# The mixer stage of a two-layer trunk: transposes by whole PSUM banks, decay matrices for two chunks at once, and other costs in the list that orders the work

## The chip, the cores and the metric

One core of one Trainium2 chip runs the whole program. The metric is the device time of one execution in microseconds. The program has five queues of instructions: PE (TensorE; its weight loads are a row of their own, PEld), DVE (VectorE), ACT (ScalarE), POOL (GpSimd) and SP (SyncE, which issues nearly all DMAs). Each queue runs in the order in which the kernel wrote it, and an instruction waits on a semaphore where it needs another engine's result.

## The reference

Layer 0 of the trunk is a state-space mixer over 256 context and 1024 latent tokens; layer 1 is an attention mixer. The change touches layer 0 alone. Its core, for each direction (forward and reversed), with tokens in chunks of 128 and heads in 8 groups `g` of 4:

```python
zc, xc, bc, cc, dtc = project(h_ctx)   # h @ in_w, a 5-tap convolution, silu
la_cum = jnp.cumsum(dtc * a, axis=2)
to_end = jnp.exp(la_cum[:, :, -1:] - la_cum) * dtc
states = jnp.einsum('bcsgn,bcsgr,bcsgrp->bcgrpn', bc, to_end, xc)
...
decay = jnp.exp(jnp.where(causal, seg, -jnp.inf))
cb = jnp.einsum('bclgn,bcsgn->bclsg', cc, bc)
w = cb[..., None] * decay * dtc[:, :, None]
y_diag = jnp.einsum('bclsgr,bcsgrp->bclgrp', w, xc)
y_off = jnp.einsum('bclgn,bcgrpn,bclgr->bclgrp', cc, prev, jnp.exp(la_cum))
```

`y_diag + y_off` of both directions, plus a skip term, is gated by `silu(z)`, normalised and multiplied by `out_w`.

## The kernel before

**Tiles.** All 1280 tokens are resident as two rounded parts, `inh` and `inl`. The projection makes 48 column tiles of 128 channels (32 that are convolved, 16 of `z`). For each it runs three token blocks of 256, 512 and 512, eight `kt` steps, and at each step three matmuls (`mm3`, lines 168 to 170: high by high, low by high, high by low), all into a `pj` bank of PSUM, of which there are two. ACT empties the bank (line 636 for a convolved tile, line 660 for `z`), four DVE taps (line 645) make the convolution, and ACT applies silu.

**A group's mix** (`mix`, one for each of the 8 groups once its tiles x0, x1, B and C are convolved) has these parts, all in plain float32 on PE:

- `trans`: for each of the ten chunks three transposes (line 690: two of x, one of B) into one `tc` bank; ACT or DVE copies x out to `xst` (lines 695, 697), ACT copies B to `Bt` (line 701). The ring `tc` has two banks.
- `state`: POOL scales x (`xw`, line 713), PE multiplies it with B (`st`, line 718), POOL decays the running state (`tm`, line 732) and DVE adds (`PV`, line 736).
- `wmat`: for one chunk, SP brings the row sums (`lab`, a ring of three tiles), POOL masks them (line 754), ACT takes eight exponentials (line 760) into W0 and W1, one for each direction; DVE adds W1 to W0 (line 773); PE makes the cross product `cb` (line 770, into a `tc` bank); DVE multiplies W0 by it (line 775). At every second chunk PE runs `diag` for both (line 795, into `yd`). W0 and W1 have two buffers each, of one chunk.
- `y_out`: PE multiplies the states with C (`yo`, line 837), DVE weighs (line 841), POOL or DVE adds (line 854), and a DMA stores.

**What sets the order.** Every step is recorded as `plan.op(engine, f, after, rank, us, takes, uses, table)`. `Plan.order` then walks a clock of its own: each engine, when it is free, takes the ready step of the lowest rank; a step is ready when its `after` steps have ended (plus `LINK`, .5 us, from another engine) and its ring has a free buffer; a step with another `table` than the engine's last costs a rank penalty and a time (`SWITCH`: 15 ranks and .2 us on PE). The result is one fixed list for each queue. The planner's times never run on the chip: there, waits come from the tiles alone. Before the change no PE step names a table.

```python
SWITCH = {"ACT": (8., 1.28), "PE": (15., .2)}
LINK, MOVE, LAND = .5, .9, 2.6
...
if any(a.end is None or a.end + (0. if a.eng == e else LINK) > now + 1e-9 for a in o.after):
    continue
```

After the mixer the program goes on with the output product, layer 1 and the final norm; their order is made by other plans, which the change leaves alone.

Of the kernel before, what the change touches and what calls it, by code (L numbers as in the profile page):

```python
# [42 lines left out]
ANY = ("tc", "wparts", "pj", "sc", "dn", "tr", "ob", "sq", "ss", "xn", "rot", "xd")  # L43
BORD = (1, 0, 9, 8, 7, 6, 5, 4, 3, 2)
# [7 lines left out]
class Plan:  # L52
# [3 lines left out]
    def __init__(self, rings):  # L56
        self.free, self.ops, self.turns, self.given = dict(rings), [], {}, {}
# [24 lines left out]
    def order(self):  # L82
# [5 lines left out]
        busy, table, moved, now, started, events = {e: 0. for e in todo}, {}, 0., 0., [], [0.]  # L88
        ends = []
        while any(todo.values()):  # L90
# [6 lines left out]
            for e, q in todo.items():  # L97
# [3 lines left out]
                for o in q:  # L101
                    if best and o.rank > best[0]:
                        break
                    if any(a.end is None or a.end + (0. if a.eng == e else LINK) > now + 1e-9 for a in o.after):
                        continue
                    if any(self.free[h.ring] <= i or h.ring not in ANY and h.n != self.given.get(h.ring, 0) + i + 1
                           for h, i in o.takes):
                        continue
                    r = o.rank + (SWITCH[e][0] if o.table and o.table != table.get(e) else 0.)
                    if best is None or r < best[0]:  # L110
                        best = (r, o)
# [4 lines left out]
                for h, _ in o.takes:  # L116
                    self.free[h.ring] -= 1
                    self.given[h.ring] = h.n
                us = o.us
                if o.table and o.table != table.get(e):  # L120
                    table[e], us = o.table, us + SWITCH[e][1]
# [7 lines left out]
                for x in (busy[e], o.end, o.end + LINK):  # L129
                    heapq.heappush(events, x)  # L130
# [15 lines left out]
def emit(tc, A, out):  # L146
# [108 lines left out]
    for b in ub:  # L255
# [5 lines left out]
                 "st": 1, "yd": 1, "yo": 1, "xst": 1, "Bt": 1, "PV": 1, "xw": 3, "tm": 1, "lab": NLAB, "W0": 2, "W1": 2, "es": 3})  # L261
# [325 lines left out]
    def load(src, after=(), rank=0., raws="wraw"):  # L587
# [18 lines left out]
        a = plan.op(*(("POOL", low, [a], rank - 30, 1.44) if odd else ("DVE", low, [a], rank - 30, .80)),  # L606
# [3 lines left out]
    def project(ct, rank):  # L610

        w = [load(A["w_in"][ct, :, h * 512:(h + 1) * 512], rank=rank + .1 * h) for h in range(2)]
        for b, (lo, hi) in enumerate(NBLK):
# [10 lines left out]
            for kt in range(KT):  # L624
                last = plan.op("PE", lambda kt=kt, f=product: f(kt), [last, w[kt // 4][2], ready_in[b, kt]], rank + .01 * b,
                               .69 if hi - lo > 256 else .36, takes=[bank] if kt == 0 else [], uses=[bank, w[kt // 4][1]])
            yield lo, hi, t, bank, last

    def conv_tile(ct, rank):
# [18 lines left out]
        for k in range(1, 5):  # L648
            a = plan.op("DVE", lambda k=k: tap(k), [a], rank - URGENT, 1.70, uses=[u, out])
# [15 lines left out]
    def mix(g, chs, rank):  # L665
# [15 lines left out]
        def trans(n, c):  # L681
            t0, bank, t = tok0(c), plan.hold("tc"), {}

            def turn():
                if n == 0:
                    s["xst"] = pool["now"].tile([128, NT, 4, 64], FT, tag="xst", name="xst")
                    s["Bt"] = pool["now"].tile([128, NT, 128], FT, tag="Bt", name="Bt")
                t["p"] = psum("tc", [128, 3, 128])
                for j, x in enumerate((x0, x1, bt)):
                    T.transpose(t["p"][:, j, :], x["a"][:, t0:t0 + 128], ident)  # L690

            def xcopy():
                xd = s["xst"][:, c].rearrange("p h d -> p (h d)")
                if n % 2 == 0:
                    S.activation(xd, flat(t["p"][:, 0:2]), AF.Copy)
                else:
                    V.tensor_copy(xd, flat(t["p"][:, 0:2]))

            a = op("PE", turn, [ax0, ax1, ab] + third, .33, takes=[bank] + ([hxst, hBt] if n == 0 else []), uses=[hx0, hx1, hb, hxst, hBt])
            b = op("DVE" if n % 2 else "ACT", xcopy, [a], .42 if n % 2 else .38, uses=[bank, hxst])  # L700
            d = op("ACT", lambda: S.activation(s["Bt"][:, c, :], t["p"][:, 2, :], AF.Copy), [a], .275, uses=[bank, hBt])
            ready[c] = (b, d)

        pv, held = [None], []

        def state(i):
            bank, t, mms = plan.hold("st"), {}, []
            for d, c in ((0, i), (1, BORD[i])):
                hw = plan.hold("xw")

                def scale(d=d, c=c):
                    t[d] = pool["now"].tile([128, 4, 64], FT, tag="xw", bufs=3, name="xw")
                    G.tensor_tensor(t[d], s["xst"][:, c], te_t[:, d, c, h4][:, :, None].to_broadcast([128, 4, 64]), op=OP.mult)  # L713

                def product(d=d, c=c):
                    if d == 0:
                        t["st"] = psum("st", [128, 2, 4, 64])
                    T.matmul(flat(t["st"][:, d]), s["Bt"][:, c, :], flat(t[d]), start=True, stop=True)  # L718

                a = op("POOL", scale, [ready[c][0], te_op], .80, takes=[hw], uses=[hxst])  # L720
                mms.append(op("PE", product, [a, ready[c][1]] + mms, .44, takes=[bank] if d == 0 else [], uses=[bank, hw, hBt]))
# [5 lines left out]
            else:  # L727
# [7 lines left out]
                a = op("POOL", decay, [pv[0]] + dec_ops, 1.11, takes=[ht], uses=[hPV])  # L735
# [3 lines left out]
        def wmat(c):  # L739

            t0, t, ws, bank = tok0(c), {}, [], plan.hold("tc")
            for d in range(2):
                hl, hw = plan.hold("lab"), plan.hold(f"W{d}")
                sgn = 1 - 2 * d

                def bring(d=d):
                    t["l", d] = pool["now"].tile([128, 4, 128], FT, tag="lab", bufs=NLAB, name="lab")
                    src = bass.AP(tensor=la_d.tensor, offset=la_d.offset + (c * 64 + d * 32 + g * 4) * 128,
                                  ap=[[0, 128], [1, 512]])
                    Q.dma_start(flat(t["l", d]), src)  # L750


                def close(d=d, sgn=sgn):
                    G.affine_select(t["l", d], t["l", d], [[0, 4], [sgn, 128]], OP.is_ge, NEVER, base=0,  # L754
                                    channel_multiplier=-sgn)

                def expo(h, d=d):
                    if h == 0:
                        t["w", d] = pool["now"].tile([128, 4, 128], FT, tag=f"W{d}", bufs=2, name="W")
                    S.activation(t["w", d][:, h], t["l", d][:, h], AF.Exp, bias=u_t[:, d, c, 4 * g + h:4 * g + h + 1])  # L760

                a = op("SP", bring, third + [la_op], .38, takes=[hl])
                a = op("POOL", close, [a], .88, uses=[hl])
                for h in range(4):
                    a = op("ACT", lambda h=h, f=expo: f(h), [a, u_op], .312, takes=[hw] if h == 0 else [], uses=[hl, hw], table="exp")
                ws.append((hw, a))

            def cross():
                t["cb"] = psum("tc", [128, 128])
                T.matmul(t["cb"], bt["a"][:, t0:t0 + 128], ct["a"][:, t0:t0 + 128], start=True, stop=True)  # L770

            b = op("PE", cross, [ab, ac], .22, takes=[bank], uses=[hb, hc])
            a = op("DVE", lambda: V.tensor_tensor(t["w", 0], t["w", 0], t["w", 1], op=OP.add), [w[1] for w in ws], .75,
                   uses=[w[0] for w in ws])
            a = op("DVE", lambda: V.tensor_tensor(t["w", 0], t["w", 0], t["cb"][:, None, :].to_broadcast([128, 4, 128]),
                                                  op=OP.mult), [a, b], .68, uses=[ws[0][0], bank])
            bi = [i for i, (c0, c1) in enumerate(BLOCKS) if c0 <= c < c1][0]
            held.append((c, t, a, ws[0][0]))
            if c % 2 == 0:
                return  # L780

            new, two = bi not in blocks, held[:]
            held.clear()
# [3 lines left out]

            def diag():
                if new:
                    bk["yd"] = [psum("yd", [128, 512]) for q in range(2)]  # L790
                for c, t, _, _ in two:
                    k = (c - bk["c"][0]) * 128
                    for h in range(4):
                        q, j = divmod(h, 2)
                        T.matmul(bk["yd"][q][j * 64:(j + 1) * 64, k:k + 128], s["xst"][:, c, h, :], t["w", 0][:, h, :], start=True,  # L795
                                 stop=True)

            bk["ops"].append(op("PE", diag, [x for c, _, w, _ in two for x in (w, ready[c][0])], 1.08, takes=[bk["h"]] if new else [],
                                uses=[bk["h"], hxst] + [x[3] for x in two]))

# [14 lines left out]
        def y_out(bi, q):  # L815
# [4 lines left out]
            for d in range(2):  # L820
# [23 lines left out]
                a = op("PE", outer, [pv[0], ac], .23 * len(cs), takes=[hy], uses=[hPV, hc])  # L844
# [3 lines left out]
                if bi == 0:  # L848
                    eng, E, us = "DVE", V, .30
# [14 lines left out]
        for n, c in enumerate(order):  # L864
            trans(n, c)
        for i in range(9):
            state(i)
            wmat(i)
# [4 lines left out]
        wmat(9)  # L873
# [13 lines left out]
    def mod_later(n, q, rank):  # L887
# [3 lines left out]
        for kt in (2 * q, 2 * q + 1):  # L891
# [13 lines left out]
            for j in both:  # L905
                done[0] = plan.op("DVE", lambda j=j, f=add: f(j), [a, done[0]], rank, .92, uses=[raw])
# [10 lines left out]
        for j in both:  # L917
# [26 lines left out]
            a = plan.op("DVE", plus, [b, done[0]], rank, .70, uses=[hr])  # L944
# [9 lines left out]
    for kind, g, q in ORDER:  # L954
# [6 lines left out]
        if q == 3:  # L961
            mix(g, chs[g], rank + 1)
    with tc.manual_schedule():
# [936 lines left out]
```

## Time and profile before

| | us |
|---|---|
| median of 3 runs | 2009.88 |
| lowest and highest run | 2005.18, 2011.53 |
| the profiled execution | 2010.66 |
| its span, first to last instruction | 2008.9 |
| granted TensorE clock in it | 0.994 |

In the profile the mixer stage reaches from the program's start to the last `yo` product at 1010 us; the first 200 us of it load, normalise and compute the step sizes, and from 200 us on the eight mixes run between the projections. Idle time of an engine is listed with what ended it. A matmul's row shows its whole passage through the array, so rows of one stream overlap: the distance from start to start is what one costs.

### The profile page before, as it was taken

Reading aid. Unit: us, or ns where it says so; the run is one execution under the profiler, and the core shown is the slowest. Engines: PE = TensorE matmul, PEld = TensorE weight load, DVE = VectorE, ACT = ScalarE, POOL = GpSimd, SP = SyncE. Lnnn points to the kernel's source line nnn. Section 1 sums busy time; section 2 is a strip of 40 time slices with the busy share of each in tenths; the row PEclk is TensorE's granted clock in tenths of the full one; section 3 lists DMA queues with packets and bytes.
Section 4 is the critical chain, followed back from the end, with each engine's and each line's share of the span. In section 5 each row is a group of like instructions: output and inputs, shape, how many; then the busy total and the mean of one; then the engine's idle time right before and its main releaser. Section 6 shows DMA issues by size and latency. Waiting matters only on the chain.

```text
span 2008.9 us, 30605 instructions
## 1 busy us (share of the span) xinstructions
PE 1949.9 (97%) x10728; PEld 1497.8 (75%) x10728; DVE 1437.8 (72%) x1737; ACT 1116.9 (56%) x2047; POOL 1189.4 (59%) x973
## 2 busy tenths in 40 slices
PE   8899999999999999999999999999999999999998
PEld 8778888888888788888878878877775444444476
DVE  1485897786959786866445788768575888888643
ACT  2446767676766677676734676534224444554521
POOL 1201776666846576856459787855265667776722
PEclk9999999999999999999999999999999999999999
DMA  6114463635372545445586686553232111111033
GB/s 244 64 32 124 132 189 115 182 100 168 112 195 91 157 125 165 141 142 158 150 278 212 212 252 196 167 153 99 74 110 90 34 41 43 43 48 32 6 105 105
DMA packets 162126, 255.50 MB, mean 127 GB/s; under 512 B 21466, under 2 KB 57178, under 8 KB 161972
## 3 DMA queue, kind: packets, MB, share of 16 engines
q1 hardware_dynamic: 160820, 251.71, 40.5%
q8 instruction: 84, 1.38, 0.3%
q10 hardware_dynamic: 1152, 1.84, 0.3%
q14 instruction: 70, 0.57, 0.1%
HBM read 210.78 MB, written 42.63 MB: 126 GB/s over the span
## 4 chain that ended last, share of the span: by engine, by line
PE 75%; DVE 9%; DMA 5%; POOL 4%; issue 3%; ACT 3%; SPq 1%; DVEq 0%; POOLq 0%; ACTq 0%
PE pj L168 8%; PE pj L169 8%; PE pj L170 8%; PE sc L1663 7%; PE ot L1679 7%; PE ob L168 7%; PE ob L170 6%; PE ob L169 6%; DVE acc L645 4%; PE yo L837 2%; PE sc L1462 2%; PE st L718 2%; DMA spare<-in_mod_w 2%; PE yd L795 2%; PE sc L168 2%
## 5 line engine op out<-in xcount | busy, mean ns | idle before, releaser
L168 PE MATMUL pj<-inh,whi 128*128 128x512 f32 (+1 forms) x1152 | 441.7, 383 | 3.9 <-DVE dv L453 3.2
L170 PE MATMUL pj<-inh,wlo 128*128 128x512 f32 (+1 forms) x1152 | 410.7, 357 | 0.0
L169 PE MATMUL pj<-inl,whi 128*128 128x512 f32 (+1 forms) x1152 | 409.9, 356 | 0.8 <-POOL inl L367 0.8
L168 PEld LDWEIGHTS pj<-inh,whi 128*128 128x128 f32 x1152 | 219.1, 190 | 32.1 <-DVE dv L453 3.6
L645 DVE SCALAR_TENSOR_TENSOR acc<-ub,convw,acc 128x1282 f32<-128x1282 f32 x128 | 230.9, 1804 | 16.3 <-ACT acc L642 13.2
L170 PEld LDWEIGHTS pj<-inh,wlo 128*128 128x128 f32 x1152 | 218.2, 189 | 32.0
L169 PEld LDWEIGHTS pj<-inl,whi 128*128 128x128 f32 x1152 | 219.4, 190 | 26.5 <-POOL inl L367 1.2
L760 ACT ACTIVATE W<-lab,u_t 128x128 f32<-128x128 f32 x640 | 202.6, 390 | 62.5 <-POOL lab L754 39.7
L754 POOL TENSOR_SCALAR_AFFINE_SELECT lab<-lab 128x512 f32<-128x512 f32 x160 | 144.8, 911 | 147.3 <-DMA lab<-la_d 141.0
L1644 POOL TENSOR_TENSOR acc<-acc,P 128x1024 f32<-128x1024 f32 x80 | 192.5, 2406 | 64.4 <-ACT P L1668 62.7
L1668 ACT ACTIVATE P<-sc 128x1024 f32<-128x1024 f32 x160 | 162.9, 1025 | 115.4 <-PE sc L1663 106.4
L1609 DVE TENSOR_REDUCE mx<-sc 128x2 f32<-128x1024 f32 (+1 forms) x140 | 167.3, 1213 | 38.3 <-PE sc L1462 37.4
L713 POOL TENSOR_TENSOR xw<-xst,te_t 128x256 f32<-128x256 f32 x144 | 143.1, 1011 | 41.5 <-PE st L718 17.8
L1679 PE MATMUL ot<-P,vv 128*64 128x512 f32 x640 | 154.8, 605 | 0.0
L602 POOL TENSOR_TENSOR wlo<-wraw,whi 128x512 fp32r<-128x512 f32 x48 | 71.7, 1493 | 126.0 <-ACT whi L599 125.8
L1663 PE MATMUL sc<-q,kh 64*128 64x512 f32 x640 | 135.9, 420 | 0.5
L170 PE MATMUL ob<-whi,yl 128*128 128x512 f32 x288 | 113.5, 394 | 1.8 <-DVE yl L1061 1.8
L168 PE MATMUL ob<-whi,yh 128*128 128x512 f32 x288 | 114.2, 397 | 0.0
L169 PE MATMUL ob<-wlo,yh 128*128 128x512 f32 x288 | 113.3, 393 | 0.0
L1663 PEld LDWEIGHTS sc<-q,kh 64*128 64x128 f32 x640 | 60.0, 184 | 69.7 <-DVE mx L1609 29.6
L902 DVE SCALAR_TENSOR_TENSOR macc<-mraw,cc,macc 128x512 f32<-128x512 f32 x98 | 102.4, 1069 | 9.9 <-DMA mraw<-in_mod_w 9.8
L732 POOL TENSOR_TENSOR tm<-PV,dec_t 128x512 f32<-128x512 f32 x64 | 92.9, 1452 | 18.3 <-DVE PV L736 17.0
(281 smaller groups left out, 4504.6 us busy)
## 6 DMA issues: line engine op xcount, KB each, us to landing
lab<-la_d SPq DMA_DIRECT2D x160, 256.0 KB
wraw<-in_w_in SPq DMA_DIRECT2D x96, 256.0 KB
workvv<-in_m_out_w SPq DMA_DIRECT2D x94, 256.0 KB
mraw<-in_mod_w SPq DMA_DIRECT2D x64, 256.0 KB
es<-e_d SPq DMA_DIRECT2D x128, 128.0 KB
wraw<-in_wqkv SPq DMA_DIRECT2D x48, 256.0 KB
spare<-in_mod_w SPq DMA_DIRECT2D x32, 256.0 KB
q_d<-qs SPq DMA_DIRECT2D x64, 128.0 KB
```

The source lines that it names most:

```text
L168: T.matmul(o, lh, rh, start=first, stop=False)
L169: T.matmul(o, lh, rl, start=False, stop=False)
L170: T.matmul(o, ll, rh, start=False, stop=last)
L645: V.scalar_tensor_tensor(t["a"], ub[i % 2][:, k:k + CW], convw[:, ct, k:k + 1], t["a"], op0=OP.mult, op1=OP.add)
L713: G.tensor_tensor(t[d], s["xst"][:, c], te_t[:, d, c, h4][:, :, None].to_broadcast([128, 4, 64]), op=OP.mult)
L754: G.affine_select(t["l", d], t["l", d], [[0, 4], [sgn, 128]], OP.is_ge, NEVER, base=0, channel_multiplier=-sgn)
L760: S.activation(t["w", d][:, h], t["l", d][:, h], AF.Exp, bias=u_t[:, d, c, 4 * g + h:4 * g + h + 1])
L1609: V.tensor_reduce(max_place(t["m"][0], i), o, AX.X, OP.max)
L1644: E.tensor_tensor(t[e], t["P", k0] if two else t[e], t["P", kt], op=OP.add)
L1663: T.matmul(o[:, h], (first_row[r] if n == 3 else (kh, kl, kh)[n][r, kv, k]), x[(0, 0, 1, 2)[n]][r], start=(n == 0), stop=(n == 3))
L1668: S.activation(t["P", kt], flat(t["s", kt]), AF.Exp)
L1679: T.matmul(t["o"][h * 64:(h + 1) * 64], vv[:, kt, kv], t["P", kt][:, h * 512:(h + 1) * 512], start=(kt == 0), stop=(kt == NT - 1))
```

## The change

1. `trans` makes five turns for x and three for B instead of ten: an x turn transposes two tiles of two chunks into one whole bank, and one copy of 512 columns empties it; a B turn takes four chunks (two in the last) and ACT copies them at once. `xst` and `Bt` now stand in the order of the transposes (`at`). An x turn no longer needs B.
2. `wmat` handles two chunks: W0 and W1 are tiles of two chunks with one buffer each, the reversed direction's exponentials stand first, one DVE add and one multiply work on 1024 columns, and one `tc` bank takes both cross products. In the plan the cross products wait for the third of the four sets of exponentials.
3. In the plan, PE steps are marked `parts` (the projection) or `whole` (the float32 steps of the mix); a change of kind costs 4 ranks and .08 us.
4. In the plan, a hand-over to PE takes 1.2 us instead of .5, the banks of ring `tc` are given out in turn (a step is not ready until the bank whose turn it is is free; before, any free bank would do in the plan), and several steps have other times: the convolution tap 1.70 to 1.8, `xw` .80 to 1.07, `tm` 1.11 to 1.5, the mask .88 to 1.0, the DVE half of a weight split .80 to 1.0, and some smaller ones.

```diff
+        self.link = {}
...
-                    if any(a.end is None or a.end + (0. if a.eng == e else LINK) > now + 1e-9 for a in o.after):
+                    if any(a.end is None or a.end + (0. if a.eng == e else self.link.get(e, LINK)) > now + 1e-9 for a in o.after):
...
-                 "st": 1, "yd": 1, "yo": 1, "xst": 1, "Bt": 1, "PV": 1, "xw": 3, "tm": 1, "lab": NLAB, "W0": 2, "W1": 2, "es": 3})
+                 "st": 1, "yd": 1, "yo": 1, "xst": 1, "Bt": 1, "PV": 1, "xw": 3, "tm": 1, "lab": NLAB, "W0": 1, "W1": 1, "es": 3})
...
-                               .69 if hi - lo > 256 else .36, takes=[bank] if kt == 0 else [], uses=[bank, w[kt // 4][1]])
+                               .69 if hi - lo > 256 else .36, takes=[bank] if kt == 0 else [], uses=[bank, w[kt // 4][1]], table="parts")
...
-            a = plan.op("DVE", lambda k=k: tap(k), [a], rank - URGENT, 1.70, uses=[u, out])
+            a = plan.op("DVE", lambda k=k: tap(k), [a], rank - URGENT, 1.8, uses=[u, out])
...
+                t[key] = psum("tc", [128, len(cs), len(tiles), 128])
+                for i, c in enumerate(cs):
+                    for j, x in enumerate(tiles):
+                        T.transpose(t[key][:, i, j, :], x["a"][:, tok0(c):tok0(c) + 128], ident)
...
-                a = op("POOL", scale, [ready[c][0], te_op], .80, takes=[hw], uses=[hxst])
+                a = op("POOL", scale, [ready[c][0], te_op], 1.07, takes=[hw], uses=[hxst])
...
-                a = op("POOL", decay, [pv[0]] + dec_ops, 1.11, takes=[ht], uses=[hPV])
+                a = op("POOL", decay, [pv[0]] + dec_ops, 1.5, takes=[ht], uses=[hPV])
...
+            done, two = [], (c0, c0 + 1)
+            for d in (1, 0):
...
+            a = op("DVE", lambda: V.tensor_tensor(t["w", 0], t["w", 0], t["w", 1], op=OP.add), done, 1.46, uses=hw)
+            b = op("PE", cross, [ab, ac, done[2]], .44, takes=[bank], uses=[hb, hc], table="whole")
+            a = op("DVE", weigh, [a, b], 1.22, uses=[hw[0], bank])
...
+    plan.switch["PE"] = (4., .08)
+    plan.link["PE"] = 1.2
```

Two places in PE's list show what this does to the order. The first is the start of group 0's mix. Before, with `tc<-ident,acc` the transposes and `pj` the projection's matmuls:

```order
L690 MATMUL tc<-ident,acc 128x128 x3
L168 MATMUL pj<-inh,whi 128x512
L169 MATMUL pj<-inl,whi 128x512
L170 MATMUL pj<-inh,wlo 128x512
L690 MATMUL tc<-ident,acc 128x128 x3
L168 MATMUL pj<-inh,whi 128x512
```

And at that place now (lines have moved: 702 is the transpose, 173 to 175 are the projection, 744 is `st`):

```order
L702 MATMUL tc<-ident,acc 128x128 x8
L173 MATMUL pj<-inh,whi 128x512
L174 MATMUL pj<-inl,whi 128x512
L175 MATMUL pj<-inh,wlo 128x512
L702 MATMUL tc<-ident,acc 128x128 x8
L173 MATMUL pj<-inh,whi 128x512
```

Two banks' worth of transposes now stand together, and three projection matmuls stand between such pairs.

The second is the last pair of chunks of group 4, with `tc<-acc` the cross product and `yo` the product with the states. Before:

```order
L837 MATMUL yo<-acc,PV 128x128
L168 MATMUL pj<-inh,whi 128x512
L169 MATMUL pj<-inl,whi 128x512
L170 MATMUL pj<-inh,wlo 128x512
L168 MATMUL pj<-inh,whi 128x256
L169 MATMUL pj<-inl,whi 128x256
L170 MATMUL pj<-inh,wlo 128x256
L770 MATMUL tc<-acc 128x128
L837 MATMUL yo<-acc,PV 128x128
```

And now (868 is `yo`, 803 the cross product):

```order
L173 MATMUL pj<-inh,whi 128x512
L174 MATMUL pj<-inl,whi 128x512
L175 MATMUL pj<-inh,wlo 128x512
L868 MATMUL yo<-acc,PV 128x128
L803 MATMUL tc<-acc 128x128 x2
L173 MATMUL pj<-inh,whi 128x512
```

Both cross products stand together now. Behind them come 18 projection matmuls before this pair's `diag`, and no other cross product. Before, at 32 of the 40 `diag` steps one or two cross products of the next pair stood ahead of the `diag`.

Over the stage PE's list has as many instructions as before. Stretches of float32 work between projection matmuls are 280 before and 243 now. ACT has 83 instructions fewer, 11 of them table loads, and DVE 104 fewer; POOL and SP have as many as before.

More of the change, by code (lines that the diff above doesn't have):

```diff
@@ L88, in order @@
         busy, table, moved, now, started, events = {e: 0. for e in todo}, {}, 0., 0., [], [0.]
+        size, out = dict(self.free), {r: [] for r in self.free}
         ends = []
@@ L679, in mix @@
         order = (0, 1, 9, 2, 8, 3, 7, 4, 6, 5)
[L681 to L690, printed above, removed]
+        at = {c: n for n, c in enumerate(order)}
@@ new lines, in trans, with turn @@
+        def trans(n):
+            t = {}
+            def turn(key, tiles, cs):
+                if not cs[0]:
+                    if key == "x":
+                        s["xst"] = pool["now"].tile([128, NT, 4, 64], FT, tag="xst", name="xst")
+                    else:
+                        s["Bt"] = pool["now"].tile([128, NT, 128], FT, tag="Bt", name="Bt")
+                t[key] = psum("tc", [128, len(cs), len(tiles), 128])
+                for i, c in enumerate(cs):
+                    for j, x in enumerate(tiles):
+                        T.transpose(t[key][:, i, j, :], x["a"][:, tok0(c):tok0(c) + 128], ident)
+            cs, bank = order[2 * n:2 * n + 2], plan.hold("tc")
+            p = op("PE", lambda: turn("x", (x0, x1), cs), [ax0, ax1, s.get("x")] + third, .45, takes=[bank] + ([] if n else [hxst]),
+                   uses=[hx0, hx1, hxst], table="whole")
+            s.setdefault("x", p)
@@ L700, in trans @@
[L700 to L704, printed above, removed]
+                    V.tensor_copy(o, i)
+            xo = op("DVE" if n % 2 else "ACT", xcopy, [p], .68 if n % 2 else .6, uses=[bank, hxst])
+            if n % 2 == 0:
+                cb, bank2 = order[2 * n:2 * n + 4], plan.hold("tc")
+                p = op("PE", lambda: turn("b", (bt,), cb), [ab, s.get("b")] + third, .11 * len(cb), takes=[bank2] + ([] if n else [hBt]),
+                       uses=[hb, hBt], table="whole")
+                s.setdefault("b", p)
+                d = op("ACT", lambda: S.activation(flat(s["Bt"][:, 2 * n:2 * n + len(cb)]), t["b"].rearrange("p c x t -> p (c x t)"),
+                                                   AF.Copy), [p], .15 * len(cb), uses=[bank2, hBt])
+                for c in cb:
+                    ready[c] = [None, d]
@@ L733, in decay @@
                                     op=OP.mult)
-                a = op("POOL", decay, [pv[0]] + dec_ops, 1.11, takes=[ht], uses=[hPV])
+                a = op("POOL", decay, [pv[0]] + dec_ops, 1.5, takes=[ht], uses=[hPV])
                 pv[0] = op("DVE", lambda: V.tensor_tensor(s["PV"][:, i], t["tm"], t["st"], op=OP.add), [a] + mms, .68,
                            uses=[ht, hPV, bank])
[L739 to L766, printed above, removed]
-            def cross():
[L769 to L783, printed above, removed]
@@ L794, in diag @@
                         q, j = divmod(h, 2)
[L795 to L799, printed above, removed]
+                        T.matmul(bk["yd"][q][j * 64:(j + 1) * 64, k:k + 128], s["xst"][:, at[c], h, :], t["w", 0][:, n, h, :],
+                                 start=True, stop=True)
+            bk["ops"].append(op("PE", diag, [a] + [ready[c][0] for c in two], 1.08, takes=[bk["h"]] if new else [],
+                                uses=[bk["h"], hxst, hw[0]], table="whole"))
         def inner(bi):
```

81 lines of the change are left out of this document (59 added, 22 removed).

## The prediction

> **What bounds the kernel now.** I read the page's first part, then busy time by stage, then PE's waits in the mixer stage, then single waits in the timeline.
>
> ```profile
> span 2008.9 us, 30605 instructions
> PE 1949.9 (97%) x10728; PEld 1497.8 (75%) x10728; DVE 1437.8 (72%) x1737; ACT 1116.9 (56%) x2047; POOL 1189.4 (59%) x973
> ```
>
> PE is busy for 97% of the span. The change reorders the mixer stage only, and of that mainly 200 to 1010 us (the row gives the stretch, its length, busy us of PE, PEld, DVE, ACT and POOL, PE's granted clock, the DMA share and GB/s):
>
> ```profile
> 200.00:1010.00 810.00, 794.66 (x4843) 677.54 (x4842) 620.86 (x722) 567.48 (x1151) 522.69 (x463) 1.00 0.49 146
> ```
>
> PE is busy there for 794.66 of 810 us at full clock, DVE for 77%, ACT 70%, POOL 65%. PE's list has the same instructions after the change, so the gain lies in what PE loses between them: 15.3 us of plain idle time, and what hides under the modelled ends of matmuls. Who ends the waits of PE's matmuls in this stretch (total, times, longest):
>
> ```profile
> PE tc L770 <- DVE W L775: 4.9, 6, 1.2
> PE st L718 <- POOL xw L713: 4.8, 5, 2.5
> PE yo L837 <- DVE es L841: 2.6, 5, 1.1
> PE st L718 <- DVE PV L736: 1.6, 3, 1.1
> PE tc L690 <- DVE xst L697: 0.7, 2, 0.4
> PE tc L690 <- ACT mr L939: 0.3, 1, 0.3
> ```
>
> And those of its weight loads:
>
> ```profile
> PEld tc L770 <- DVE W L775: 8.9, 12, 1.6
> PEld st L718 <- POOL xw L713: 7.0, 6, 2.9
> PEld yo L837 <- DVE es L841: 5.3, 7, 1.5
> PEld st L718 <- DVE PV L736: 3.7, 6, 1.4
> PEld tc L690 <- DVE xst L697: 1.5, 2, 0.8
> PEld tc L690 <- ACT Bt L701: 1.0, 4, 0.4
> PEld tc L690 <- ACT mr L939: 0.5, 1, 0.5
> ```
>
> They sum to 14.9 us in 22 waits by the matmuls and 27.9 us in 38 by the weight loads. All are short and all stand before float32 work; none names the projection. One of them in the timeline, the cross product of group 4 whose rows are in the section on the change:
>
> ```profile
> 668.76 0.69 DVE L773 TENSOR_TENSOR W<-W 128x512 f32<-128x512 f32 x1 [2.76 <-ACT W L760]
> 668.83 0.28 PE L169 MATMUL pj<-inl,whi 128*128 128x256 f32 x1
> 668.95 0.28 PE L170 MATMUL pj<-inh,wlo 128*128 128x256 f32 x1
> 669.49 0.69 DVE L775 TENSOR_TENSOR W<-W,tc 128x512 f32<-128x512 f32 x1
> 670.23 0.49 PE L770 MATMUL tc<-acc 128*128 128x128 f32 x2 [1.00 <-DVE W L775]
> ```
>
> A 256-column matmul costs .12 us from start to start (668.83 to 668.95), so PE was free at 669.07 and began at 670.23: 1.16 us lost, where the matmul's wait says 1.00. The truth lies between the two sums; I take the middle, **21.4 us** as the whole prize in this stretch. The wait is for the bank of an earlier cross product, which line 775 releases at 670.18; PE starts .05 us later. So a hand-over itself is cheap, and the wait comes from a DVE that ran late against the plan.
>
> **Kept together: the price of a change of kind.** The next rows are PE's: three and six transposes between projection matmuls.
>
> ```profile
> 620.85 0.49 PE L690 MATMUL tc<-ident,acc 128*128 128x128 f32 x3
> 621.09 0.48 PE L168 MATMUL pj<-inh,whi 128*128 128x512 f32 x1
> 621.41 0.39 PE L169 MATMUL pj<-inl,whi 128*128 128x512 f32 x1
> 621.64 0.39 PE L170 MATMUL pj<-inh,wlo 128*128 128x512 f32 x1
> ...
> 611.34 0.82 PE L690 MATMUL tc<-ident,acc 128*128 128x128 f32 x6
> 611.91 0.48 PE L168 MATMUL pj<-inh,whi 128*128 128x512 f32 x1
> 612.23 0.40 PE L169 MATMUL pj<-inl,whi 128*128 128x512 f32 x1
> ```
>
> From the first transpose to the second projection matmul it is .56 us with three and .89 us with six: .11 for each transpose. Take three transposes (.33) off .56, and .23 is left for L168, which is what a 512-column matmul of the stream costs (621.41 to the next at 621.64), so a change of kind costs at most .02 us. The list has 37 float32 stretches fewer: 37 x .02 = .7 us at most; I take .4. This part of the change hardly does what its name says.
>
> **Later and better-timed hand-overs.** A float32 step now enters PE's list .7 us later against its producer (1.2 instead of .5). If each wait were to shrink by up to .7 us, the matmuls' waits would lose 6 x .7 + 5 x .7 + 2.6 + 1.6 + .7 + .3 = 12.9 us, the weight loads' 12 x .7 + 6 x .7 + 7 x .7 + 3.7 + 1.4 + 1.0 + .5 = 24.1 us; the middle is 18.5. (Classes whose mean is under .7 are counted as gone, so this leans high.) The producers' times in the plan also come nearer to these rows, the costs of one in ns behind the comma:
>
> ```profile
> L645 DVE SCALAR_TENSOR_TENSOR acc<-ub,convw,acc 128x1282 f32<-128x1282 f32 x128 | 230.9, 1804 | 16.3 <-ACT acc L642 13.2
> L713 POOL TENSOR_TENSOR xw<-xst,te_t 128x256 f32<-128x256 f32 x144 | 143.1, 1011 | 41.5 <-PE st L718 17.8
> L732 POOL TENSOR_TENSOR tm<-PV,dec_t 128x512 f32<-128x512 f32 x64 | 92.9, 1452 | 18.3 <-DVE PV L736 17.0
> ```
>
> The old plan believed 1.70, .80 and 1.11 us. It left POOL short by 144 x .21 + 64 x .34 = 52 us over the stage, and DVE's taps by 13 us; the new one is within .06 of each. So the largest late producer, `xw` with its 2.5 us wait, should be met too, and I need no discount for it.
>
> The new list will have waits of its own, because a pair's work arrives in larger pieces. I give back a third of the 18.5, 6 us, between nothing and all of it: the row nearest to it is the cross product's own, which is 4.9 of the 14.9 us.
>
> **Pairs and whole banks.** The sizes of the pieces, from the groups of this stretch:
>
> ```profile
> L773 DVE TENSOR_TENSOR W<-W 128x512 f32<-128x512 f32 x78 | 67.1, 860 | 39.2 <-ACT W L760 39.1
> L775 DVE TENSOR_TENSOR W<-W,tc 128x512 f32<-128x512 f32 x78 | 53.3, 685 | 3.5 <-PE tc L770 1.4
> L701 ACT ACTIVATE Bt<-tc 128x128 f32<-128x128 f32 x80 | 19.8, 276 | 8.9 <-PE tc L690 5.9 <-DVE xst L697 2.9
> L697 DVE COPY xst<-tc 128x256 f32<-128x256 f32 x40 | 16.1, 415 | 12.5 <-PE tc L690 8.2 <-ACT Bt L701 4.2
> L695 ACT ACTIVATE xst<-tc 128x256 f32<-128x256 f32 x40 | 15.2, 379 | 14.5 <-PE tc L690 14.5
> ```
>
> The new 1024-column add costs between .86 and 1.72 us, the multiply between .69 and 1.37, an x copy between .38 and .83, a B copy of four chunks between .28 and 1.10; I take the upper ends, the sizes doubled or fourfold. Then DVE and ACT have no more work than now, at best some 60 and 20 us less. Both have 190 us or more of slack in this stretch, so I count 0 for it. Without that cover it would be worth those sums. SP issues the same 160 `lab` loads into the same three tiles and POOL runs the same masks, so their queues only shift: 0.
>
> The single W0 and W1 buffers add a real wait on ACT. For W0 it is hardly new: a `diag` reads two chunks, so both old buffers came free together too. Queued behind a waiting exponential are the evictions of `pj` (line 636), for which PE would wait next; the two banks cover 24 matmuls x .23 = 5.5 us. I count 0, and price the loss of that cover below. The reversed direction's eight exponentials now come ahead of the wait for W0, which speaks for less waiting.
>
> The first 200 us keep their loads. The one PE wait there that the mixer's plan could move is this one:
>
> ```profile
> PE pj L168 <- DVE dv L453: 3.2, 1, 3.2
> ```
>
> In the new list four taps still stand before that `dv` on DVE: 0, within 3 us either way.
>
> **The sum:** -18.5 + 6 - .4 = -12.9 us on the span of 2008.9 us. The execution itself took 2010.66, .8 above the median of 2009.88; on the median the sum gives **1997 us**. A measurement of this kernel can tell a difference of about 0.3%, 6 us, from none.
>
> **Rivals.** *The waits move to the `tc` banks: 2010 us.* Eight transposes now fill both banks, and three projection matmuls (.68 us) stand before the next eight. A turn takes .44 us and its copy up to .83. The first bank is then free at 1.27 us, where PE returns to it at .87 + .68 = 1.55; the second has to be free at 1.99 and is, at 1.7, if its copy runs on the other engine, but not until 2.1 behind the first copy. A table load ahead of it makes PE late by about a microsecond. If that meets one in six of 64 turns, at 1.28 us a load (the row below), it is 64 x 1.28 / 6 = 13.7 us, which eats the gain.
>
> ```profile
> L760 ACT ACT_TABLE_LOAD x57 | 73.1, 1283 | 3.2 <-issue 1.1 <-DVE W L773 0.7 <-DVE W L775 0.5
> ```
>
> For it speaks how closely the turns stand; against it that 80 turns now cost PE only .7 us behind copies of x, though they stand as closely, and that the plan now gives the banks out in turn. The Trainium skill has a rule that speaks against the change here: "Perfetto Trace Analysis", under Matmuls in Optimizing Tensor Performance, says that independent matmul groups should rotate through different PSUM banks so that emptying one overlaps the next group's matmuls. By that rule bigger turns over the same two banks would overlap less, and the time would be this rival's; the present waits of L690 are too small to show it.
>
> *ACT is held by the single W0: 2031 us, slower.* ACT now stands this long for `diag`:
>
> ```profile
> ACT W L760 <- PE yd L795: 20.1, 12, 4.7
> ```
>
> Its mean is 1.7 us, and no PE wait names an eviction, so the banks cover it. In the new list up to some 13 us of PE work stand between a pair's cross product and its `diag`; if ACT reaches W0 early, it holds the evictions behind it, and from 5.5 us on PE starves. At 40 pairs and half of 1.7 us each that is +34 us, less the 13 gained: +21. Against it: the list makes ACT take W1 first, and other steps can go ahead of W0 in the plan, which knows when W0 comes free.
>
> *The weight loads tell the truth and nothing is given back:* -24.1 - .7 - 3.2 = -28 gives 1982 us.
>
> **Chances.** Forecast, 1988 to 2003.9: 0.57. Under 1988: 0.04. Waits move, 2003.9 to 2016: 0.24. Held by W0, above 2016: 0.15. Hence faster by over 0.3% 0.61, within it 0.24, slower 0.15. The range 1988 to 2016 leaves out 0.19.
>
> **What would show it.** In the new profile PE's idle time from 200 us to the last `yo` should fall from 15.3 us to about 7, the last `yo` should come about 12 us earlier, and waits of `st` for `xw` and of the cross product for line 775's successor should nearly vanish. Rows `tc <- xst` or `tc <- Bt` of several us would be the first rival; PE `pj` behind an eviction, with ACT waiting for `yd` well above 20 us, the second. Everything behind 1010 us should keep its length; if it doesn't, a boundary effect that I left out decides.

## The result, and the profile after

| | before | after |
|---|---|---|
| median, 6 runs each (us) | 2010.08 | 1998.84 |
| lowest and highest run | 2005.18, 2011.53 | 1996.22, 2001.03 |
| ratio of the medians, 95% interval | | 0.995 [0.9939, 0.996] |
| the profiled execution | 2010.66 | 1998.06 |
| idle time of PE, 200 to 1010 us | 15.3 | 8.2 |
| matmul waits in the mixer, 200 us to its end | 14.9 in 22 | 7.8 in 14 |
| last `yo` product begins | 1009.87 | 997.15 |

The change makes the program 11.2 us faster, and all six runs after lie below all six before. The head of the page after:

```profile
span 1996.3 us, 30365 instructions
PE 1944.4 (97%) x10728; PEld 1495.3 (75%) x10728; DVE 1434.0 (72%) x1633; ACT 1099.2 (55%) x1964; POOL 1214.6 (61%) x973
```

PE has the same 10728 matmuls, and its share looks as it did. The gain is in the stretch that the prediction read; busy time by stage, same columns as there:

```profile
200.00:1010.00 810.00, 801.83 (x4873) 685.39 (x4872) 616.71 (x625) 551.40 (x1067) 540.12 (x461) 1.00 0.49 149
```

In this stretch PE did 30 matmuls more than before and stood idle for 8.2 us. Behind the last `yo` projection matmuls still follow: 45 of 512 columns before, 48 of 512 and 15 of 256 after. So some 2.4 of the 12.7 us by which the last `yo` comes earlier are projection work that now stands behind it, and what was won is read at the first output product, in the timelines of before and of after (start, length, PE):

```profile
1020.23 0.40 PE L168 MATMUL tr<-whi,yh 128*128 128x512 f32 x1
```

```profile
1009.96 0.40 PE L173 MATMUL tr<-whi,yh 128*128 128x512 f32 x1
```

Of the 12.6 us between the two profiled executions, 10.3 are won by here; behind it the program took 988.7 and 986.4 us to the end of the span. That last stretch has the same list and took between 984.3 and 990.4 us over all the profiles of this study without following the mixer's end, so its 2.3 us are no effect that can be put down to the change.

PE's matmul waits after (total, times, longest):

```profile
PE st L744 <- DVE PV L763: 3.6, 6, 1.1
PE yo L868 <- DVE es L872: 3.4, 5, 1.1
PE tc L702 <- DVE xst L715: 0.4, 1, 0.4
PE tc L702 <- ACT Bt L723: 0.2, 1, 0.2
PE st L744 <- ACT PV L752: 0.2, 1, 0.2
```

Cross products (4.9 us before) and `st` behind `xw` (4.8) wait no more. What has grown are the waits in which PE is held by a PSUM buffer of which the plan has one: `st` until `PV` has emptied it (1.6 to 3.6), `yo` until `es` has (2.6 to 3.4). One of them in the timeline:

```profile
398.99 2.48 DVE L650 SCALAR_TENSOR_TENSOR acc<-ub,convw,acc 128x1282 f32<-128x1282 f32 x1
...
400.07 1.86 POOL L739 TENSOR_TENSOR xw<-xst,te_t 128x256 f32<-128x256 f32 x1
...
400.73 0.39 PE L175 MATMUL pj<-inh,wlo 128*128 128x512 f32 x1
401.38 0.68 DVE L763 TENSOR_TENSOR PV<-tm,st 128x512 f32<-128x512 f32 x1
...
402.12 0.70 PE L744 MATMUL st<-xw,Bt 128*128 128x256 f32 x2 [0.99 <-DVE PV L763]
```

A tap of 2.48 us stands ahead of `PV` on DVE where the plan counts 1.8; `PV` ends at 402.06, the bank is free, and PE starts .06 us later. The `st` did not wait for its data: by POOL's order its own two `xw` had ended by 397.60. The `xw` beside that tap, which is for the next state, took 1.86 us where the plan counts 1.07. In the plan a bank is free the moment its last user ends, whatever `link` says: the later hand-over is applied to the steps in `after`, not to the buffers in `takes`.

The two feared places, ACT's wait for `diag` and the new pieces' sizes (groups: total, ns of one, idle before):

```profile
ACT W L790 <- PE yd L826: 3.8, 3, 1.9
```

```profile
L809 DVE TENSOR_TENSOR W<-W 128x1024 f32<-128x1024 f32 x40 | 59.7, 1493 | 26.3 <-ACT W L790 26.3
L807 DVE TENSOR_TENSOR W<-W,tc 128x1024 f32<-128x1024 f32 x40 | 48.8, 1219 | 4.9 <-PE tc L803 1.7 <-PE pj L175 0.5
L713 ACT ACTIVATE xst<-tc 128x512 f32<-128x512 f32 x21 | 12.5, 593 | 15.8 <-PE tc L702 15.8
L723 ACT ACTIVATE Bt<-tc 128x512 f32<-128x512 f32 x14 | 7.5, 589 | 7.7 <-PE tc L702 7.7
```

ACT waits for `diag` 3.8 us in 3 waits instead of 20.1 in 12. The add on two chunks costs 1.493 us against 2 x .860, the multiply 1.219 against 2 x .685, and both copies lie inside the bounds of the prediction.

### The profile page after: what moved, and what is told of

Its sections match the earlier page's. It is cut to its first block, busy times and chain, and to the rows that moved or that the text cites. A ratio compares the mean times of both kernels' runs of the same rounds, so it can differ in the third digit from the quotient of the medians.

```text
span 1996.3 us, 30365 instructions
## 1 busy us (share of the span) xinstructions
PE 1944.4 (97%) x10728; PEld 1495.3 (75%) x10728; DVE 1434.0 (72%) x1633; ACT 1099.2 (55%) x1964; POOL 1214.6 (61%) x973
## 4 chain that ended last, share of the span: by engine, by line
PE 78%; DVE 7%; DMA 5%; issue 3%; ACT 3%; POOL 2%; SPq 2%; DVEq 0%; POOLq 0%; ACTq 0%
PE pj L173 8%; PE pj L174 8%; PE pj L175 8%; PE sc L1696 7%; PE ot L1712 7%; PE ob L173 7%; PE ob L175 6%; PE ob L174 6%; DVE acc L650 3%; PE st L744 3%; PE yo L868 2%; PE sc L1495 2%; PE yd L826 2%; PE sc L173 2%; PE sc L175 2%
## 5 line engine op out<-in xcount | busy, mean ns | idle before, releaser
L784 POOL TENSOR_SCALAR_AFFINE_SELECT lab<-lab 128x512 f32<-128x512 f32 x160 | 155.3, 978 | 119.7 <-DMA lab<-la_d 104.2
L739 POOL TENSOR_TENSOR xw<-xst,te_t 128x256 f32<-128x256 f32 x144 | 149.4, 1050 | 37.8 <-PE st L744 31.8
L607 POOL TENSOR_TENSOR wlo<-wraw,whi 128x512 fp32r<-128x512 f32 x48 | 77.4, 1613 | 125.4 <-ACT whi L604 125.4
L933 DVE SCALAR_TENSOR_TENSOR macc<-mraw,cc,macc 128x512 f32<-128x512 f32 x98 | 107.2, 1123 | 7.2 <-DMA mraw<-in_mod_w 7.0
```

The lines of the kernel that those rows point to most:

```text
L739: G.tensor_tensor(t[d], s["xst"][:, at[c]], te_t[:, d, c, h4][:, :, None].to_broadcast([128, 4, 64]), op=OP.mult)
L784: G.affine_select(t["l", d, k], t["l", d, k], [[0, 4], [sgn, 128]], OP.is_ge, NEVER, base=0, channel_multiplier=-sgn)
```

## The experiments

The result is what was forecast, but the forecast put four edits into one sum. So the question was which of them pays. The change is taken apart into **pairs** (whole-bank transposes and decay matrices for two chunks), **times** (eight new durations in the plan: tap, `xw`, `tm`, mask, weight split, the small `es` add, and `macc` and `plus`, two DVE steps of the modulation) and **rules** (the longer hand-over `link`, the banks of `tc` given out in turn, the marks `parts` and `whole` with their price). Every variant computes the full result. Each was compared with the kernel before on the same chip; in the three groups of runs (e1 to e4, e5 to e8, e9 to e12) its median was 2009.49, 2009.16 and 2009.53 us. All together, with "waits" the sum of PE's matmul waits in the mixer from 200 us on and "mixer" the start of the first output product, both from one profile:

| | pairs | times | rules | median us | ratio, 95% | waits us | mixer us |
|---|---|---|---|---|---|---|---|
| before | | | | 2010.08 | 1 | 14.9 | 1020.2 |
| e1_pairs_only | x | | | 2010.77 | 1.0008 [0.9999, 1.0016] | 19.4 | 1024.8 |
| e8_single_times | | x | | 1997.8 | 0.9943 [0.993, 0.9955] | 7.0 | 1006.7 |
| e5_pairs_times | x | x | | 1993.6 | 0.9918 [0.9905, 0.9932] | 3.7 | 1001.9 |
| e2_plan_only | | x | x | 2016.93 | 1.0034 [1.0022, 1.0046] | 19.5 | 1026.5 |
| e7_old_times | x | | x | 2024.94 | 1.0072 [1.0058, 1.0086] | 25.8 | 1034.5 |
| **after** | x | x | x | 1998.84 | 0.995 [0.9939, 0.996] | 7.8 | 1010.0 |
| e3_no_link | x | x | no link | 2000.03 | 0.9951 [0.9939, 0.9963] | 6.9 | 1008.2 |
| e4_no_turns | x | x | no turns | 1997.74 | 0.9939 [0.9927, 0.9952] | 8.1 | 1009.0 |
| e6_no_marks | x | x | no marks | 1997.0 | 0.9938 [0.9926, 0.9951] | 5.0 | 1008.5 |
| e11_pairs_times_link | x | x | link alone | 1996.88 | 0.994 [0.9928, 0.9952] | 4.8 | 1005.1 |
| e9_single_pool_times | | `xw`, `tm` | | 2007.43 | 0.9991 [0.9981, 1.0001] | 12.1 | 1018.9 |
| e10_single_other_times | | the other six | | 2002.65 | 0.9969 [0.9957, 0.9981] | 12.9 | 1013.7 |
| e12_pairs_times_bank | x | x | banks free later | 1988.12 | 0.9894 [0.9881, 0.9907] | 2.9 | 998.6 |

**e1_pairs_only**: the change without its new rules and times.

```diff
-ROUND = ("tc", "y")
+ROUND = ()
...
-    plan.switch["PE"] = (4., .08)
-    plan.link["PE"] = 1.2
```

(and no `table=` on PE's steps, and the eight old times).

> The new code for whole banks and pairs, with the old planner: hand-over .5 us, no turns for the banks of tc, no marks on PE steps, old times. Theory A (my prediction: later hand-overs and truer times make the gain, pairs and banks add nothing): 2010 us, within 3. Theory B (the gain is the cross product alone: in pairs it no longer stands ahead of another pair's diag and no longer waits for a tc bank that line 775 holds): about 2000 us, the waits of the cross product for DVE W near 0, those of st for xw still 4 to 7 us. Theory C (the banks of tc given out in turn in the plan make it): 2009 us, the cross product still waits.

It is no faster than before. PE's waits in it:

```profile
PE st L744 <- POOL xw L739: 8.9, 10, 1.3
PE st L744 <- DVE PV L762: 5.2, 5, 1.5
PE yd L825 <- DVE W L806: 3.7, 6, 1.3
PE yo L867 <- DVE es L871: 1.6, 3, 0.9
```

The cross products' 4.9 us are gone, as the pairs should have it; but `st` waits for `xw` 8.9 us instead of 4.8, and `yd` now waits for the larger multiply. Larger pieces in a plan with the old times move the waits and add to them: 19.4 us instead of 14.9. In this profile the mixer ends 4.6 us later than before, and the stretch behind it took 984.3 us instead of 988.7. Theory B, which expected 2000 us, is out.

**e2_plan_only**: the kernel before with times and rules, `trans` and `wmat` as they were.

```diff
+    plan.switch["PE"] = (4., .08)
+    plan.link["PE"] = 1.2
...
-                a = op("POOL", scale, [ready[c][0], te_op], .80, takes=[hw], uses=[hxst])
+                a = op("POOL", scale, [ready[c][0], te_op], 1.07, takes=[hw], uses=[hxst])
```

(with the seven other times, the turns of `tc` and the marks).

> The old code for transposes and single chunks, with the whole new planner: hand-over 1.2 us, banks of tc in turn, marks, new times. A: about 1999 us. B: 2006 to 2010 us, since 31 of 40 diags still have a later cross product ahead of them. C: about 2000 us.

It is slower than before, where the prediction's 18.5 us would have had it clearly faster:

```profile
PE tc L775 <- DVE W L780: 5.3, 3, 3.6
PE yo L842 <- DVE es L846: 5.0, 6, 1.6
PE pj L173 <- ACT ub L641: 2.5, 2, 2.1
```

The cross product still waits for line 780 to free its bank, now up to 3.6 us at a time. Theories A and C, with 1999 and 2000 us for this list, are out as well.

**e3_no_link**, **e4_no_turns** and **e6_no_marks** each take one rule out of the change:

```diff
-    plan.link["PE"] = 1.2
```

```diff
-ROUND = ("tc", "y")
+ROUND = ()
```

```diff
-            b = op("PE", cross, [ab, ac, done[2]], .44, takes=[bank], uses=[hb, hc], table="whole")
+            b = op("PE", cross, [ab, ac, done[2]], .44, takes=[bank], uses=[hb, hc])
...
-    plan.switch["PE"] = (4., .08)
```

(the marks are taken off all PE steps, the cross product stands for them).

> The changed kernel with the hand-over to PE back at .5 us in the plan. A: 2005 to 2009 us, with waits of st, yo and transposes back at some 10 us. B: 1999 us, within 3. C: 1999 us.

> The changed kernel without the rule that the banks of tc are given out in turn. A: 1999 to 2001 us. B: 1999 us, within 3. C: 2009 us, with waits of transposes and cross products for copies and line 807.

> The changed kernel without the marks on PE's steps (no penalty for a change of kind). D: 1999 us, within 3, though its list has 264 float32 stretches where the changed kernel has 243. E: 2006 to 2011 us.

All three lie within 2 us of the change, and their intervals overlap its interval: none of the rules alone carries the gain. With the longer hand-over taken away, the waits it was meant to shorten do not come back:

```profile
PE yo L868 <- DVE es L872: 3.8, 7, 1.3
PE st L744 <- DVE PV L763: 2.8, 5, 1.0
```

They are the two bank waits again, 6.6 us against 7.0 in the change; without the turns they are 7.3. Without the marks most of them are gone:

```profile
PE yo L867 <- DVE es L871: 1.3, 4, 0.4
PE st L744 <- DVE PV L762: 0.7, 1, 0.7
```

So of the three rules it is the marks with which the bank waits come, though the time without them is only 1.8 us less, which does not stand clear of the noise. The list without marks has 264 stretches of float32 work instead of 243 and is no slower, so 21 changes of kind together cost too little to be seen here.

**e5_pairs_times** has the pairs and the eight times and none of the rules, **e8_single_times** the kernel before with the eight times and nothing else, and **e7_old_times** the change with the eight old times. The edit of e8; e7's is the same backwards on the kernel after:

```diff
-            a = plan.op("DVE", lambda k=k: tap(k), [a], rank - URGENT, 1.70, uses=[u, out])
+            a = plan.op("DVE", lambda k=k: tap(k), [a], rank - URGENT, 1.8, uses=[u, out])
...
-                a = op("POOL", scale, [ready[c][0], te_op], .80, takes=[hw], uses=[hxst])
+                a = op("POOL", scale, [ready[c][0], te_op], 1.07, takes=[hw], uses=[hxst])
...
-                a = op("POOL", decay, [pv[0]] + dec_ops, 1.11, takes=[ht], uses=[hPV])
+                a = op("POOL", decay, [pv[0]] + dec_ops, 1.5, takes=[ht], uses=[hPV])
...
-                a = op("POOL", close, [a], .88, uses=[hl])
+                a = op("POOL", close, [a], 1.0, uses=[hl])
```

(and DVE's half of a weight split .80 to 1.0, the small `es` add .30 to .40, `macc` .92 to 1.05, `plus` .70 to 1.1).

> The new code for whole banks and pairs with the new times alone; hand-over .5 us, no turns for tc, no marks. Theory D (two things are needed together: pairs take away the cross product's waits, and true times for POOL and DVE keep the waits of st for xw and of diag for W from taking their place): 1996 to 2002 us, waits of st for xw under 2 us and of the cross product near 0. Theory E (the marks that keep float32 work together make it, with the pairs): 2007 to 2011 us, and it keeps the waits that e1 showed.

> The changed kernel with the eight old times (tap 1.70, xw .80, tm 1.11, mask .88 and so on); hand-over 1.2, turns and marks kept. D: 2004 to 2011 us, with the waits of st for xw back at 5 to 9 us. E: 1999 us. If the longer hand-over alone can cover late producers, it is under 2003 too.

> The kernel before with the eight new times alone. D: 2004 to 2012 us: st waits less for xw, the cross product as much as before or more. If true times alone make the gain, about 1999 us.

Eight numbers that never run on the chip make the kernel before 11 us faster, as much as the whole change (e8). Without them the change is 15 us slower than before (e7), which no theory had expected. Without the rules it is 5 us faster than with them (e5). So theory E is out, and D too, since the times alone make the gain that it gave to times and pairs together.

All eight old times are too short by the profile of before, and all were raised, but not all are nearer to it now. Five are: tap, `xw`, `tm`, `macc` (1.07 us there) and `plus` (1.18). The other three went past it and are no nearer than they were: the mask took .91 us there (old plan .88, new 1.0), DVE's half of a weight split .89 (.80, 1.0), the small `es` add .32 (.30, .40). So e8 shows what longer times are worth; whether they must be the measured ones, or whether any margin on these steps would do, no run here tells.

The waits of e7:

```profile
PE st L744 <- DVE PV L763: 20.8, 22, 2.6
PE yo L868 <- DVE es L872: 2.9, 4, 1.1
```

With old times and the rules, `st` waits 22 times and 20.8 us in all for `PV` to empty the single `st` bank: the wait for `xw` (8.9 in e1) is gone, and four times the bank wait has come in its place. And the waits of e8 and of e5:

```profile
PE tc L770 <- DVE W L775: 2.5, 5, 1.0
PE pj L168 <- ACT ub L636: 1.8, 1, 1.8
```

```profile
PE st L744 <- POOL xw L739: 3.1, 6, 1.0
PE yo L867 <- DVE es L871: 0.6, 1, 0.6
```

In e8 the cross products still wait half as long as before (2.5 of 4.9); in e5 the pairs have taken that away, and the time falls by another 4 us.

**e9_single_pool_times** and **e10_single_other_times** split e8 into the two times of POOL and the six others.

> The kernel before with POOL's two new times alone (xw 1.07, tm 1.5). Theory F (of the eight times, POOL's two make the gain, since xw ends the largest waits and the old plan left POOL 52 us short): 1996 to 2001 us, waits of st for xw under 1 us. Theory G (the six others, the taps above all, make it): 2007 to 2012 us.

> The kernel before with the six other new times (tap 1.8, mask 1.0, weight split 1.0 and so on), xw and tm as before. F: 2005 to 2011 us, waits of st for xw as before or more. G: 1996 to 2001 us.

The two of POOL alone can't be told from no change; the six others make about 7 us of the 11, and POOL's two on top of them the remaining 4 to 5. Theory F is out; G named the right six but expected all of the gain from them. The waits of e10 and of e9:

```profile
PE tc L770 <- DVE W L775: 3.7, 4, 2.5
PE st L718 <- POOL xw L713: 2.9, 4, 1.1
```

```profile
PE yo L837 <- DVE es L841: 4.3, 9, 1.0
PE st L718 <- POOL xw L713: 3.1, 5, 1.1
PE tc L770 <- DVE W L775: 2.0, 5, 0.8
```

Where only POOL's are raised, `st` waits less for `xw` and the cross product waits less, but `yo` waits longer for `es`; only both together bring all three down (e8).

**e11_pairs_times_link** and **e12_pairs_times_bank** put a margin into e5, in two places. e11 adds the later hand-over. e12 adds it where the hand-over doesn't reach: in the plan the banks of `tc`, `st`, `yd` and `yo` come free .6 us after their last user.

```diff
+    plan.link["PE"] = 1.2
```

```diff
+BANK, BANKS = .6, ("tc", "st", "yd", "yo")
...
-                for h in heapq.heappop(ends)[2].holds:
+                for h in heapq.heappop(ends)[3]:
...
-                heapq.heappush(ends, (o.end, o.n, o))
+                for late in (0., BANK):
+                    heapq.heappush(ends, (o.end + late, o.n, late, [h for h in o.holds if (h.ring in BANKS) == (late > 0.)]))
```

> e5 (pairs and new times, 1993.6 us) with the hand-over to PE at 1.2 us. Theory H (the longer hand-over costs: in the plan a bank comes free without any hand-over, so waits for banks of st and yo grow while those for data shrink): 1997 to 2001 us, waits of st for DVE PV and of yo for DVE es of 2 us and more each. If the hand-over is harmless and the turns or the marks cost, 1992 to 1996 us.

> e5 with the margin put where H says that it is missing: in the plan the PSUM banks of tc, st, yd and yo come free .6 us after their last user's end; hand-over .5 us. H: 1988 to 1993 us, waits of st for PV and yo for es near 0 (e5 has 0 and .6 us), so at most some 2 us under e5. If margins cost by themselves, wherever they stand: 1995 to 2000 us.

The hand-over costs e5 3.3 us (1996.88; the lowest of its five runs, 1993.73, reaches into e5's 1989.92 to 1994.39). The margin on the banks gains 5.5 us, and e12 is the fastest of all: 21 us under before, 10.7 under the change. Waits in e11:

```profile
PE pj L173 <- ACT ub L641: 2.1, 1, 2.1
PE tc L702 <- DVE xst L715: 1.0, 2, 0.7
PE st L744 <- DVE PV L762: 1.0, 2, 0.7
PE yo L867 <- DVE es L871: 0.4, 1, 0.4
```

In e12:

```profile
PE st L746 <- POOL xw L741: 2.3, 2, 1.5
PE yo L869 <- DVE es L873: 0.6, 1, 0.6
```

Theory H's times came out (e11's just below its range), but not its waits of 2 us each: the bank waits that are 7.0 us in the change are 1.4 in e11, so the hand-over is not by itself what makes them. And e12's waits are only .8 us below e5's, while it gained 3.3 us by the first output product: the matmul waits of one profile show the direction, not all of the gain.

## Why the prediction came out, point by point

- **The prize and where it lies: right.** All that can be told was won in the mixer, 10.3 us by the first output product. The matmuls' waits fell by 7.1 us (14.9 to 7.8), those of the weight loads for other engines by 11.8 (28.1 to 16.3). The prediction took the middle of the two sums as the truth, and the middle of the two falls, 9.5 us, is near to what was won. Over all the lists the time rises with the matmuls' waits, from 2.9 us at 1988 to 25.8 at 2025: a straight line through the 14 gives about 1.4 us for each and leaves single lists up to 4 us away.
- **A change of kind at .02 us at most, .4 in all: right as far as it can be told.** The list of e6 has 21 stretches more and is not slower; .02 us each is too little for these runs to confirm.
- **"Later and better-timed hand-overs", 18.5 us: the step that failed.** It took the later hand-over as the cause (each wait .7 us shorter) and the better times as the reason to expect no discount. The runs turn that round. The times alone make 11 us (e8); the hand-over makes nothing that can be told in the change (e3) and costs 3 in e5 (e11). Together the rules cost in all three places where they can be compared: 19 us on single chunks with the new times (e8 to e2), 14 on pairs with the old times (e1 to e7), 5 on pairs with the new ones (e5 to after). The flaw is in the step itself: moving a PE step .7 us later shortens its own wait only if nothing else holds it, and a step that waits for a bank is not moved by `link` at all. The matmuls' waits `st <- PV` and `yo <- es` stood in the prediction's rows and were counted as gone; they grew from 4.2 to 7.0 us.
- **`xw` as the largest late producer: fell.** POOL's two times, 52 us of the plan's error, made nothing that can be told alone (e9); the six others, among them DVE's taps at 13 us, made 7 (e10). The size of a duration's error over the stage does not say what mending it is worth.
- **Pairs and whole banks at 0: right alone, wrong in company.** e1 can't be told from before. On top of the new times they are worth 4.2 us (e8 to e5), and within the change's rules 18 (e2 to after).
- **Six microseconds given back: right in kind, and named from the wrong row.** New waits came, but with the new times they go with the marks and not with the pairs' larger pieces: the bank waits are 7.0 us in the change, 2.0 without its marks (e6) and .6 with the pairs and no rule (e5); on single chunks 5.7 with the rules (e2) and 1.4 without (e8).
- **The rivals.** The waits did not move to the `tc` banks: .4 and .2 us, so two banks with whole-bank turns are enough here. The rule on rotating groups through different banks, in the Trainium skill's "Perfetto Trace Analysis", section Matmuls in Optimizing Tensor Performance, would have had them grow, as the prediction read it; the rows show no such cost. ACT was not held by the single W0: 3.8 us instead of 20.1. That the reversed direction's exponentials stand first may be the reason; no run turns their order round. No list reached the 1982 us of the weight loads.
- **What would show it.** Idle time to about 7 us (8.2), the last `yo` some 12 us earlier (12.7, of which 2.4 are projection work moved behind it), the waits of `st` for `xw` and of the cross product gone: all seen. Those signs belong to the times and the pairs as well as to the hand-over, so they could not tell the causes apart; only the runs did.
- One count ahead of the prediction is off by one: a cross product of the next pair stood ahead of the `diag` at 31 of the 40 steps, not 32.

So the number was right by luck, in so far as its largest term had the wrong cause: a loss from the rules (5 us) and a gain from the times and the pairs (16) ended near the sum of other terms.

**What stays open.** Each variant is one list, and lists that differ by one rule differ by some 2 us for no reason that a row shows; effects of that size (link, turns or marks singly in the change) are not settled. Whether the eight times work because they are nearer to the profile or because they are longer was not tested. Neighbours in the table (e8 and e5, e5 and e12) have intervals that touch at their ends. Why the three rules together cost 5 us on e5, while taking any one of them out of the change moves it by less than 2, and why e12 gains more than its shown waits, was not found. How the marks bring the bank waits about was not followed through the plan either.

## What to carry to other kernels

Where a fixed list is made by a plan, first raise the durations that the profile shows to be too short, all of them at once, before changing what it schedules: here that was worth as much as the whole change, and larger pieces paid only after it. A margin belongs where the plan has none: find which waits a new margin can reach (here not those for a single bank) before giving it a price. And when several edits enter one term of a sum, a right total says nothing of the parts.

## What was not expected of the hardware

One duration for a step is a mean over two cases. The same instruction after, by its line (shortest, median and longest in ns):

```profile
L739 POOL TENSOR_TENSOR xw<-xst,te_t x144: 605/992/1867, 182.3 to 947.6; 128x256 f32<-128x256 f32 x144
```

```profile
L650 DVE SCALAR_TENSOR_TENSOR acc<-ub,convw,acc x128: 1537/1787/2617, 103.7 to 924.1; 128x1282 f32<-128x1282 f32 x128
```

From 200 us on, the 42 `xw` that lie at least half of their time beside a tap have a median of 1.86 us, the 93 others one of .62. The plan's 1.07 lies between the two cases, and ahead of the wait at 402 us above stands a meeting of a long tap with a long `xw`. The Trainium skill, "SBUF — State Buffer", section "SBUF: two separate sides", says that a DVE instruction with two inputs in SBUF and a GpSimd instruction that reads SBUF take one pair of ports as an exclusive lock: the one that starts first holds it for the whole instruction, and the other blocks. The tap reads `ub` and `acc`, `xw` reads `xst`, and the long cases agree with it. No run here removed either partner, so the cause is argued and not shown.
